# First projections of the retention layer: four whole tiles instead of five, the last tile's products bank by bank, banks emptied in a written order, decay tables behind

## The chip, the cores and the metric

The kernel runs on one core of a Trainium2 chip. The core has a matrix engine (TensorE, in the profile PE, its weight loads PEld), a vector engine (VectorE, DVE), a scalar engine (ScalarE, ACT), GpSimd (POOL) and SyncE (SP), which here issues nearly all transfers. Products land in eight banks of PSUM, which only PE, DVE and ACT reach. The metric is the device time of one execution in microseconds; lower is better.

## The reference

Two layers of a generator over latent tokens (256) with a context (256 tokens) through the same weights. Layer 0 mixes tokens by retention with four heads, layer 1 by neighbourhood attention; each is followed by a SwiGLU. The width is 1024. What matters here is the very beginning of layer 0: the adaLN modulation of the input and the projections of the first head.

```
m_lat = jnp.split(cond_lat @ ada_w[i] + ada_b[i], 6, axis=-1)
m_ctx = jnp.split(cond_ctx @ ada_w[i] + ada_b[i], 6, axis=-1)
a_lat = modulate(h_lat, m_lat[0], m_lat[1])
a_ctx = modulate(h_ctx, m_ctx[0], m_ctx[1])
...
q, k, v, g = jnp.split(a @ w_in, [hk, 2 * hk, 2 * hk + hv], axis=-1)
if rope is not None:
    q, k = apply_rope(q, *rope), apply_rope(k, *rope)
k = k * RET_DK ** -0.5
...
decay = lambda lg: jnp.broadcast_to(lg[None, :, None, None], (B, RET_HEADS, n, RET_DK))
```

Only latents are rotated (rope); the scan in both directions is computed as scores times a table of decays, then times the values, and the gate g goes through SiLU.

## The kernel before

**Tiles and operands.** The input stands transposed: eight tiles kt of 128 features by 512 tokens, 256 latents and then 256 of context. For each kt the program computes scale and shift of these 128 features for both streams, four passes of `ada.column` on DVE (L225: 1024 elements by the condition, summed into one column), then on ACT the modulated tile `am` (L408, one half per stream) and its rounded copy `aT[kt][0]` (L413). Products are made in float32r, an fp32 rounded so that PE takes it in one pass; to keep the precision, each operand is split into a high part (the rounded copy, made by ACT) and a low part (the rest, a subtraction on DVE), and a product is three of them: high by high, high by low, low by high (`mm3`, L138 to L142). `low(kt)` (L343) makes the low part of the input tile.

**First projections.** Weight unit kt (128 by 1024) of the first eight holds the first head's q and k columns (four blocks of 128) and v columns (512) for the features of tile kt. All eight banks are taken: `qk_ps[0..3]` for q (two) and k (two), transposed, and `v_ps[0..3]` for v, by tokens. Every tile adds to all eight banks, so no bank is final before the last tile. Tiles below `WHOLE`, which is 5, use the unsplit fp32 operands (`whole_products`, L345 to L354), one stream at a time, as soon as `am` is there. For the others ACT makes the high part of the weights (L402), DVE the low part (L359) and the input's low part, and `split_products` (L356 to L369) issues eight high by high products, one for each bank, and then the two others for each bank in turn. In the loop, the split products of tile kt − 1 stand behind the columns of tile kt. The last tile's stand behind the loop, and behind them the low parts of the whole tiles, which later projections need.

**Order.** `tc.manual_schedule` keeps the instructions written inside it in that order on the engines that it names; here all five. It ends after the low parts (L424). Everything else is ordered by the framework's scheduler, and `tc.issue_after(ins)` puts instructions of the same engine behind one. Loads on SP for the next tile are written at the top of each turn: adaLN rows, weights, input. Weight units share three buffers (`raw`), so a load waits until a buffer has been read. The stream of later units (`Stream`, L85 to L133) loads, casts on ACT (L123) and makes low parts on DVE (L124); unit 8 is the first of the gate projection.

**Behind the region, before.** Five tables are loaded (L426 to L430: distances `dlt`, decays `lg`, the cosines and sines, and the layer norms' columns), behind the weight load of tile 6. `decay_prep` and `decay_table` make for each head two tables of 128 by 384 decays: four exponentials on ACT (L457, L462), three products or sums on GpSimd (L458, L459, L463); heads 1, 2 and 3 are stored to DRAM (L465) and loaded again later, and head 0's stays in the one buffer `Dt`. They stand behind the last tile's cast (`lasts[-1]`). `qk_evac` empties two banks: four products with cosine and sine on DVE (L488), two copies of the context half on ACT (L493, L496), a difference and a sum (L497, L498), and the split. `v_evac` splits the four v banks. In the program's text the first head's q, k and v banks are emptied only after all functions have been defined, in front of `proj_g(0)`, the gate projection, whose first bank is one that has been emptied. Then come the scaled input z through the two buffers `pf` (L805, L806), which the decay tables use as well, and the heads: `scores`, where DVE multiplies by the table into `pf` (L554, L558), the next head's q and k, and `values`.

Of the kernel before, what the change touches and what calls it, by code (L numbers as in the profile page):

```python
# [8 lines left out]
F32 = mybir.dt.float32  # L9
F32R = mybir.dt.float32r  # L10
BF16 = mybir.dt.bfloat16
AF = mybir.ActivationFunctionType
ALU = mybir.AluOpType
# [5 lines left out]
P = 128  # L19
D = 1024  # L20
KT = D // P
NLAT = 256
NCTX = 256
NTOK = NLAT + NCTX
# [9 lines left out]
CTX_FIRST = (2, 3, 0, 1)  # L34
# [10 lines left out]
def backbone(ctx: ExitStack, tc: tile.TileContext, wpack, adapack, cond, condcol, xT, xtok, adab, lncol, lnrow,  # L45
# [271 lines left out]
    with Phase("ret", "yTh", "yTl", "vh", "vl", "kh", "kl") as rp:  # L317
# [17 lines left out]
            xts[kt] = rp.tile([P, NTOK], F32, tag=f"yT{'hl'[kt % 2]}{kt // 2 % 2}", name=f"xt{kt}")  # L335
            nc.sync.dma_start(xts[kt], xT[kt])

        WHOLE = 5
        ams = {}
        split_ops = {}  # L340

        def low(kt):
            nc.vector.tensor_tensor(out=aT[kt][1], in0=ams[kt], in1=aT[kt][0].bitcast(F32), op=ALU.subtract)  # L343
# [12 lines left out]
        def split_products(kt):  # L356

            raw, u = split_ops.pop(kt)
            nc.vector.tensor_tensor(out=u[1], in0=raw, in1=u[0].bitcast(F32), op=ALU.subtract)  # L359
            low(kt)  # L360
            outs = [(qk_ps[f], cut(u, slice(None), slice(f * P, f * P + P)), aT[kt]) for f in range(4)]
            outs += [(v_ps[t], cut(aT[kt], slice(None), slice(t * P, t * P + P)), cut(u, slice(None), slice(512, 1024)))
                     for t in CTX_FIRST]
            last = kt == KT - 1
            for o, x, m in outs:
                nc.tensor.matmul(o, x[0], m[0], start=False, stop=False)
            for o, x, m in outs:
                nc.tensor.matmul(o, x[0], m[1], start=False, stop=False)
                nc.tensor.matmul(o, x[1], m[0], start=False, stop=last)  # L369

        ORD = ("axw", "awx")
        REG = {PE, DVE, POOL, ACT, SP}
# [13 lines left out]
        for kt in range(KT):  # L386
            if kt + 1 < KT:
                for f in ORD[kt > 0]:
                    if f == "w":
                        stream.load_to(kt + 2)  # L390
                    elif f == "x":
                        load_x(kt + 1)
                    else:
                        ada.load_to(2 * kt + 4)

            am = ams[kt] = rp.tile([P, NTOK], F32, tag=f"v{'hl'[kt % 2]}{CTX_FIRST[kt // 2]}", name=f"am{kt}")
            raw = stream.raw.pop(kt)
            stream.split = stream.used = kt + 1
            if kt >= WHOLE:
                u = (wsplit.tile([P, UNIT], F32R, tag="whi", name=f"whi{kt}", bufs=stream.BUFS),  # L400
                     wsplit.tile([P, UNIT], F32R, tag="wlo", name=f"wlo{kt}", bufs=stream.BUFS))
                nc.scalar.copy(u[0], raw)  # L402
                split_ops[kt] = raw, u
            for s in range(2):
                sl = slice(s * NLAT, s * NLAT + NLAT)
                for i in (2 * kt, 2 * kt + 1):
                    ada.column(i, s)
                nc.scalar.activation(am[:, sl], xts[kt][:, sl], AF.Identity,  # L408
                                     bias=adacol[0][s][:, kt:kt + 1], scale=adacol[0][s][:, 8 + kt:9 + kt])
            ada.tiles.pop(2 * kt)  # L410
            ada.tiles.pop(2 * kt + 1)
            ada.done += 2
            lasts.append(nc.scalar.copy(aT[kt][0], am))  # L413
            if kt < WHOLE:
                whole_products(kt, raw)

            if kt - 1 in split_ops:
                split_products(kt - 1)
            if kt == WHOLE:
                tables_after = stream.last_load.ins  # L420
        split_products(KT - 1)
        for kt in range(WHOLE):
            low(kt)
        region.__exit__(None, None, None)  # L424
        with tc.issue_after(tables_after):
            nc.sync.dma_start(dlt, delta)  # L426
            nc.sync.dma_start(lg, decay.partition_broadcast(P))
            nc.sync.dma_start(cosT, rope[0])
            nc.sync.dma_start(sinT, rope[1])
            nc.sync.dma_start(lnc, lncol)  # L430

        dp = [rp.tile([P, 384], F32, tag=tg, name=f"dp{i}") for i, tg in enumerate(("g2", "yTl2", "sqsum"))]
        lgw = rp.tile([P, 2, 8], F32, name="lgw")

        def decay_prep():
            nc.scalar.activation(lg, lg, AF.Exp)
            nc.gpsimd.tensor_scalar(out=lg, in0=lg, scalar1=-1.0, scalar2=0.0, op0=ALU.mult, op1=ALU.add)
            nc.gpsimd.tensor_scalar(out=lgw[:, 0], in0=lg, scalar1=256.0, scalar2=0.0, op0=ALU.mult, op1=ALU.add)  # L440
            nc.gpsimd.tensor_scalar(out=lgw[:, 1], in0=lg, scalar1=-1.0, scalar2=0.0, op0=ALU.mult, op1=ALU.add)
            nc.scalar.activation(dp[0], dlt, AF.Relu)
            nc.scalar.activation(dp[1], dlt, AF.Relu, scale=-1.0)

            nc.gpsimd.memset(dp[2], 1.0)
            nc.gpsimd.affine_select(out=dp[2], in_=dp[2], compare_op=ALU.not_equal, fill=2.0, base=-128,
                                    pattern=[[1, 384]], channel_multiplier=-1)

        def load_decay(h):
            Dt[h] = rp.tile([P, 2, 384], F32, tag="Dt", name=f"Dt{h}")  # L450
            nc.sync.dma_start(Dt[h], dscr[h])

        def decay_table(h):
            D_ = rp.tile([P, 2, 384], F32, tag="Dt", name=f"Dw{h}")
            e = [rp.tile([P, 384], F32, tag=f"yT{'hl'[i]}3", name=f"de{i}_{h}") for i in range(2)]
            for i in range(2):
                nc.scalar.activation(e[i], dp[i], AF.Exp, scale=lg[:, 4 * i + h:4 * i + h + 1])  # L457
            nc.gpsimd.tensor_tensor(out=e[0], in0=e[0], in1=e[1], op=ALU.mult)  # L458
            nc.gpsimd.tensor_tensor(out=D_[:, 1, :], in0=e[0], in1=dp[2], op=ALU.mult)  # L459
            x = [rp.tile([P, NTOK], F32, tag="pf", name=f"dx{i}_{h}", bufs=2)[:, 0:384] for i in range(2)]  # L460
            for i, rate in enumerate((lg[:, h:h + 1], lgw[:, 1, 4 + h:5 + h])):
                nc.scalar.activation(x[i], dlt, AF.Exp, scale=rate, bias=lgw[:, 0, 4 * i + h:4 * i + h + 1])  # L462
            nc.gpsimd.tensor_tensor(out=D_[:, 0, :], in0=x[0], in1=x[1], op=ALU.add)  # L463
            if h:
                nc.sync.dma_start(dscr[h], D_)  # L465
            else:
                Dt[h] = D_

        with tc.issue_after(lasts[-1].ins):
            decay_prep()  # L470
            for h in (1, 2, 3, 0):
                decay_table(h)

        qk = {}
        vv = {}
        gg = {}
        yT = {}
        Pp = {}

        def qk_evac(h, which, ps):  # L480

            f = rp.tile([P, 2, NTOK], F32, tag="qf", name=f"qf{h}{which}", bufs=1)
            scale = 1.0 / 16.0 if which == "q" else 1.0
            m = [rp.tile([P, NLAT], F32, tag=f"rm{i}", name=f"rm{i}_{h}{which}") for i in range(2)]
            x = [f[:, i, 0:NLAT] for i in range(2)]

            def times(o, i, table):
                nc.vector.scalar_tensor_tensor(out=o, in0=ps[i][:, 0:NLAT], scalar=scale, in1=table, op0=ALU.mult,  # L488
                                               op1=ALU.mult)

            times(x[0], 0, cosT)
            times(m[1], 0, sinT)
            nc.scalar.activation(f[:, 0, NLAT:], ps[0][:, NLAT:], AF.Copy, scale=scale)  # L493
            times(x[1], 1, cosT)
            times(m[0], 1, sinT)
            nc.scalar.activation(f[:, 1, NLAT:], ps[1][:, NLAT:], AF.Copy, scale=scale)  # L496
            nc.vector.tensor_tensor(out=x[0], in0=x[0], in1=m[0], op=ALU.subtract)  # L497
            nc.vector.tensor_tensor(out=x[1], in0=m[1], in1=x[1], op=ALU.add)  # L498
            pr = (rp.tile([P, 2, NTOK], F32R, tag=f"{which}h", name=f"{which}h{h}"),
                  rp.tile([P, 2, NTOK], F32R, tag=f"{which}l", name=f"{which}l{h}"))  # L500
            split_into(pr, f)
            qk[(h, which)] = pr

        def v_evac(h, ps):
            for t in CTX_FIRST:
                pr = (rp.tile([P, 512], F32R, tag=f"vh{t}", name=f"vh{t}_{h}"),
                      rp.tile([P, 512], F32R, tag=f"vl{t}", name=f"vl{t}_{h}"))
                split_into(pr, ps[t])
                vv[(h, t)] = pr

        def proj_qk(h):
            for which in "qk":
# [280 lines left out]
        def fam_of(pool, tag="fam", w=256, bufs=2):  # L793
            return lambda n, i, name: pool.tile([P, w], F32, tag=tag, name=name, bufs=bufs)[:, :n]

        for i, w in ((0, "q"), (2, "k")):
            qk_evac(0, w, qk_ps[i:i + 2])
        v_evac(0, v_ps)
        proj_g(0)
        for t in CTX_FIRST:  # L800
            for half in range(2):
# [605 lines left out]
```

## Time and profile before

| | |
|---|---|
| median of 3 runs | 1184.1 us (1179.56 to 1184.3) |
| profiled execution | 1185.73 us, its span 1184.0 us |
| mean granted clock of PE | 0.993 of full speed |
| busy: PE, PEld, DVE, ACT, POOL | 1157.6, 963.9, 785.0, 455.3, 291.8 us |
| all weight loads | 228 of 512 KB, median 3.7 us from issue to landing |

A row of a timeline gives the start in the span, the duration, the engine, the line of the kernel, the operation, what it writes and reads with partitions and elements, and how many were merged; in brackets the idle time of the engine before it and what ended that. A row of the list of waits gives who waited for whom, the total, how often, and the longest. A row of a window gives its stretch and length, the busy time and count of each engine asked for, the granted clock of PE, the share of the transfer engines, and GB/s. A matmul's duration holds its pipeline; from start to start it is shorter.

### The profile page before, as it was taken

Reading aid. Unit: us, or ns where it says so; the run is one execution under the profiler, and the core shown is the slowest. Engines: PE = TensorE matmul, PEld = TensorE weight load, DVE = VectorE, ACT = ScalarE, POOL = GpSimd, SP = SyncE. Lnnn points to the kernel's source line nnn. Section 1 sums busy time; section 2 is a strip of 40 time slices with the busy share of each in tenths; the row PEclk is TensorE's granted clock in tenths of the full one; section 3 lists DMA queues with packets and bytes.
Section 4 is the critical chain, followed back from the end, with each engine's and each line's share of the span. In section 5 each row is a group of like instructions: output and inputs, shape, how many; then the busy total and the mean of one; then the engine's idle time right before and its main releaser. Section 6 shows DMA issues by size and latency. Waiting matters only on the chain. (4 is left out here: it accounts for less than half of the span.)

```text
span 1184.0 us, 15315 instructions
## 1 busy us (share of the span) xinstructions
PE 1157.6 (98%) x5670; PEld 963.9 (81%) x5670; DVE 785.0 (66%) x1131; ACT 455.3 (38%) x714; POOL 291.8 (25%) x281
## 2 busy tenths in 40 slices
PE   7999999999999998999999999999999998999997
PEld 5778888888888887888888888887888877888886
DVE  7987957645745589667776476555355577778645
ACT  3582423332433253232212233135354465566530
POOL 0054214104203567000131000015444434300000
PEclk9999999999999999999999999999999999999999
DMA  8755554233334223456546677426488743777650
GB/s 325 275 204 209 161 196 138 90 126 128 133 107 131 83 72 110 170 103 246 205 163 208 173 261 246 148 67 128 152 224 258 205 140 117 245 232 224 209 170 36
DMA packets 70010, 201.72 MB, mean 170 GB/s; under 512 B 14512, under 2 KB 17072, under 8 KB 69936
## 3 DMA queue, kind: packets, MB, share of 16 engines
q1 hardware_dynamic: 69648, 200.23, 53.0%
q8 instruction: 44, 0.72, 0.3%
q10 hardware_dynamic: 288, 0.52, 0.1%
q14 instruction: 30, 0.25, 0.1%
HBM read 187.98 MB, written 2.25 MB: 161 GB/s over the span
## 5 line engine op out<-in xcount | busy, mean ns | idle before, releaser
L124 DVE TENSOR_TENSOR wlo<-raw,whi 128x1024 fp32r<-128x1024 f32 x220 | 289.5, 1320 | 209.2 <-ACT whi L123 202.8
L123 ACT CAST whi<-raw 128x1024 fp32r<-128x1024 f32 x220 | 229.7, 1049 | 462.9 <-PE f L141 122.8
L225 DVE CUSTOM_DVE_ANT_0 junk<-adaraw,cond,adab_sb 128x1024 bf16<-128x1024 f32 x160 | 216.4, 1352 | 48.8 <-DMA adaraw<-in_adapack 46.3
L141 PE MATMUL f<-aT,whi 128*128 128x512 f32 (+1 forms) x384 | 143.7, 374 | 4.8 <-DVE aT L756 4.7
L142 PE MATMUL f<-aT,wlo 128*128 128x512 f32 (+1 forms) x384 | 143.3, 373 | 0.0
L140 PE MATMUL f<-aT,whi 128*128 128x512 f32 (+1 forms) x384 | 143.1, 373 | 0.0
L851 PE MATMUL f<-aT,whi 128*128 128x512 f32 x320 | 112.9, 397 | 0.0
L313 POOL TENSOR_TENSOR pb_n<-pa_n,mhalf 128x1 f32<-128x1 f32 x12 | 8.4, 702 | 347.8 <-DVE pa_n L312 347.8
L852 PE MATMUL f<-aT,wlo 128*128 128x256 f32 x320 | 90.0, 282 | 0.3 <-DVE wlo L124 0.3
L141 PEld LDWEIGHTS f<-aT,whi 128*128 128x128 f32 x384 | 72.9, 190 | 18.2 <-DVE aT L756 5.5
L140 PEld LDWEIGHTS f<-aT,whi 128*128 128x128 f32 x384 | 73.0, 190 | 12.6
L142 PEld LDWEIGHTS f<-aT,wlo 128*128 128x128 f32 x384 | 73.0, 190 | 12.5
L851 PEld LDWEIGHTS f<-aT,whi 128*128 128x128 f32 x320 | 60.0, 188 | 14.4
L140 PE MATMUL d<-whi,hh 128*128 128x512 f32 x176 | 68.6, 389 | 0.0
L142 PE MATMUL d<-whi,hl 128*128 128x512 f32 x176 | 68.5, 389 | 0.0
L141 PE MATMUL d<-wlo,hh 128*128 128x512 f32 x176 | 68.5, 389 | 0.0
L142 PE MATMUL v<-whi,aT 128*128 128x512 f32 x160 | 63.0, 395 | 1.8 <-POOL aT L756 1.8
L622 POOL TENSOR_TENSOR z<-t,z 128x512 f32<-128x512 f32 x28 | 44.4, 1595 | 76.0 <-DVE t L620 75.9
L140 PE MATMUL v<-whi,aT 128*128 128x512 f32 x160 | 62.8, 393 | 0.0
L141 PE MATMUL v<-wlo,aT 128*128 128x512 f32 x160 | 62.8, 392 | 0.0
L852 PEld LDWEIGHTS f<-aT,wlo 128*128 128x128 f32 x320 | 60.3, 189 | 0.8 <-DVE wlo L124 0.7
L140 PE MATMUL g<-aT,whi 128*128 128x512 f32 x128 | 50.7, 396 | 1.9 <-ACT qf0q L493 1.9
(286 smaller groups left out, 2436.8 us busy)
## 6 DMA issues: line engine op xcount, KB each, us to landing
raw<-in_wpack SPq DMA_DIRECT2D x228, 512.0 KB, 3.7
adaraw<-in_adapack SPq DMA_DIRECT2D x96, 512.0 KB, 4.5
ln<-in_lnrow SPq DMA_DIRECT2D x16, 256.0 KB, 4.5
braw<-in_rpb SPq DMA_DIRECT2D x8, 512.0 KB, 5.3
kh<-sth SPq DMA_DIRECT2D x32, 128.0 KB, 3.0
kl<-stl SPq DMA_DIRECT2D x32, 128.0 KB, 2.4
gateb<-gscr SPq DMA_DIRECT2D x6, 512.0 KB, 6.3
xt<-in_xT SPq DMA_DIRECT2D x8, 256.0 KB, 4.6
```

Source lines behind the costliest of these rows:

```text
L123: nc.scalar.copy(hi, raw)
L124: self.last_low = nc.vector.tensor_tensor(out=lo, in0=raw, in1=hi.bitcast(F32), op=ALU.subtract)
L140: nc.tensor.matmul(o, s[0], m[0], start=start, stop=False)
L141: nc.tensor.matmul(o, s[0], m[1], start=False, stop=False)
L142: nc.tensor.matmul(o, s[1], m[0], start=False, stop=stop)
L225: nc.vector.tensor_tensor_reduce(out=junk, in0=self.tiles[i], in1=condb[s], scale=1.0, scalar=adab_sb[:, l, m:m + 1], op0=ALU.mult, op1=AL ...
L313: nc.gpsimd.tensor_tensor(out=b, in0=a, in1=mhalf[:, 0:n], op=ALU.pow)
L622: eng.tensor_tensor(out=z[t][:, cs], in0=t2, in1=z[t][:, cs], op=ALU.add)
L851: nc.tensor.matmul(b[i].rearrange("p (a t) -> p a t", a=2), st[0], m, start=kt == 0, stop=False)
L852: nc.tensor.matmul(b[i][:, 0:NLAT], st[1], m[:, 0, :], start=False, stop=kt == KT - 1)
```

## The change

`WHOLE` becomes 4: tile 4 is split as well, and its split products stand behind the columns of tile 5. The last tile's products are issued bank by bank, all three of one bank in a row, in the order q, q, k, k, v of tokens 2, 3, 0, 1. The table loads move into the loop, behind the loads for tile 7 and with units 8 and 9 ahead of the columns of the norms. The region goes on after the last products with an order written out: unit 8's split, the low parts of the four whole tiles, `decay_prep`, the table of head 1, and the two q banks; between q's copies and its sums stand the four v banks and unit 9's split. The tables of heads 2, 3 and 0 come behind q's second copy on ACT. The k banks are emptied outside the region, as before.

```
-        WHOLE = 5
+        WHOLE = 4
...
             last = kt == KT - 1
+            if last:
+                for o, x, m in outs:
+                    mm3(o, x, m, False, True)
+                return
...
-        def qk_evac(h, which, ps):
+        def qk_evac(h, which, ps, between=None):
...
-            nc.scalar.activation(f[:, 1, NLAT:], ps[1][:, NLAT:], AF.Copy, scale=scale)
+            copy = nc.scalar.activation(f[:, 1, NLAT:], ps[1][:, NLAT:], AF.Copy, scale=scale)
+            if between:
+                between(copy)
...
-            if kt == WHOLE:
-                tables_after = stream.last_load.ins
+            if kt == KT - 2:
+                nc.sync.dma_start(dlt, delta)
+                nc.sync.dma_start(lg, decay.partition_broadcast(P))
+                nc.sync.dma_start(cosT, rope[0])
+                nc.sync.dma_start(sinT, rope[1])
+                stream.load_to(KT + 2)
+                nc.sync.dma_start(lnc, lncol)
         split_products(KT - 1)
+        stream.split_to(KT + 1)
         for kt in range(WHOLE):
             low(kt)
+        decay_prep()
+        decay_table(1)
+        decay_after = []
+        def first_values(copy):
+            v_evac(0, v_ps)
+            stream.split_to(KT + 2)
+            decay_after.append(copy.ins)
+        qk_evac(0, "q", qk_ps[0:2], first_values)
         region.__exit__(None, None, None)
-        with tc.issue_after(tables_after):
-            nc.sync.dma_start(dlt, delta)
...
-        with tc.issue_after(lasts[-1].ins):
-            decay_prep()
-            for h in (1, 2, 3, 0):
+        with tc.issue_after(decay_after[0]):
+            for h in (2, 3, 0):
                 decay_table(h)
...
-        for i, w in ((0, "q"), (2, "k")):
-            qk_evac(0, w, qk_ps[i:i + 2])
-        v_evac(0, v_ps)
+        qk_evac(0, "k", qk_ps[2:4])
         proj_g(0)
```

`decay_prep`, `decay_table`, `load_decay`, `v_evac` and the rest of `qk_evac` move up in the text, unchanged.

More of the change, by code (lines that the diff above doesn't have):

```diff
@@ L368, in split_products, with decay_prep @@
                 nc.tensor.matmul(o, x[0], m[1], start=False, stop=False)
-                nc.tensor.matmul(o, x[1], m[0], start=False, stop=last)
+                nc.tensor.matmul(o, x[1], m[0], start=False, stop=False)
+        dp = [rp.tile([P, 384], F32, tag=tg, name=f"dp{i}") for i, tg in enumerate(("g2", "yTl2", "sqsum"))]
+        lgw = rp.tile([P, 2, 8], F32, name="lgw")
+        def decay_prep():
+            nc.scalar.activation(lg, lg, AF.Exp)
+            nc.gpsimd.tensor_scalar(out=lg, in0=lg, scalar1=-1.0, scalar2=0.0, op0=ALU.mult, op1=ALU.add)
+            nc.gpsimd.tensor_scalar(out=lgw[:, 0], in0=lg, scalar1=256.0, scalar2=0.0, op0=ALU.mult, op1=ALU.add)
+            nc.gpsimd.tensor_scalar(out=lgw[:, 1], in0=lg, scalar1=-1.0, scalar2=0.0, op0=ALU.mult, op1=ALU.add)
+            nc.scalar.activation(dp[0], dlt, AF.Relu)
+            nc.scalar.activation(dp[1], dlt, AF.Relu, scale=-1.0)
+            nc.gpsimd.memset(dp[2], 1.0)
+            nc.gpsimd.affine_select(out=dp[2], in_=dp[2], compare_op=ALU.not_equal, fill=2.0, base=-128,
+                                    pattern=[[1, 384]], channel_multiplier=-1)
@@ new lines, in load_decay, with decay_table @@
+        def load_decay(h):
+            Dt[h] = rp.tile([P, 2, 384], F32, tag="Dt", name=f"Dt{h}")
+            nc.sync.dma_start(Dt[h], dscr[h])
+        def decay_table(h):
+            D_ = rp.tile([P, 2, 384], F32, tag="Dt", name=f"Dw{h}")
+            e = [rp.tile([P, 384], F32, tag=f"yT{'hl'[i]}3", name=f"de{i}_{h}") for i in range(2)]
+            for i in range(2):
+                nc.scalar.activation(e[i], dp[i], AF.Exp, scale=lg[:, 4 * i + h:4 * i + h + 1])
+            nc.gpsimd.tensor_tensor(out=e[0], in0=e[0], in1=e[1], op=ALU.mult)
+            nc.gpsimd.tensor_tensor(out=D_[:, 1, :], in0=e[0], in1=dp[2], op=ALU.mult)
+            x = [rp.tile([P, NTOK], F32, tag="pf", name=f"dx{i}_{h}", bufs=2)[:, 0:384] for i in range(2)]
+            for i, rate in enumerate((lg[:, h:h + 1], lgw[:, 1, 4 + h:5 + h])):
+                nc.scalar.activation(x[i], dlt, AF.Exp, scale=rate, bias=lgw[:, 0, 4 * i + h:4 * i + h + 1])
+            nc.gpsimd.tensor_tensor(out=D_[:, 0, :], in0=x[0], in1=x[1], op=ALU.add)
+            if h:
+                nc.sync.dma_start(dscr[h], D_)
+            else:
+                Dt[h] = D_
@@ new lines, in backbone, with times @@
+        qk = {}
+        vv = {}
+        gg = {}
+        yT = {}
+        Pp = {}
+        def qk_evac(h, which, ps, between=None):
+            f = rp.tile([P, 2, NTOK], F32, tag="qf", name=f"qf{h}{which}", bufs=1)
+            scale = 1.0 / 16.0 if which == "q" else 1.0
+            m = [rp.tile([P, NLAT], F32, tag=f"rm{i}", name=f"rm{i}_{h}{which}") for i in range(2)]
+            x = [f[:, i, 0:NLAT] for i in range(2)]
+            def times(o, i, table):
+                nc.vector.scalar_tensor_tensor(out=o, in0=ps[i][:, 0:NLAT], scalar=scale, in1=table, op0=ALU.mult,
+                                               op1=ALU.mult)
+            times(x[0], 0, cosT)
+            times(m[1], 0, sinT)
+            nc.scalar.activation(f[:, 0, NLAT:], ps[0][:, NLAT:], AF.Copy, scale=scale)
+            times(x[1], 1, cosT)
+            times(m[0], 1, sinT)
+            copy = nc.scalar.activation(f[:, 1, NLAT:], ps[1][:, NLAT:], AF.Copy, scale=scale)
+            if between:
+                between(copy)
+            nc.vector.tensor_tensor(out=x[0], in0=x[0], in1=m[0], op=ALU.subtract)
+            nc.vector.tensor_tensor(out=x[1], in0=m[1], in1=x[1], op=ALU.add)
+            pr = (rp.tile([P, 2, NTOK], F32R, tag=f"{which}h", name=f"{which}h{h}"),
+                  rp.tile([P, 2, NTOK], F32R, tag=f"{which}l", name=f"{which}l{h}"))
+            split_into(pr, f)
+            qk[(h, which)] = pr
@@ L371, in backbone, with v_evac @@
+        def v_evac(h, ps):
+            for t in CTX_FIRST:
+                pr = (rp.tile([P, 512], F32R, tag=f"vh{t}", name=f"vh{t}_{h}"),
+                      rp.tile([P, 512], F32R, tag=f"vl{t}", name=f"vl{t}_{h}"))
+                split_into(pr, ps[t])
+                vv[(h, t)] = pr
         ORD = ("axw", "awx")
@@ L437, in decay_prep @@
[L437 to L467, printed above, removed]
@@ L469, in backbone @@
-        with tc.issue_after(lasts[-1].ins):
-            decay_prep()
-            for h in (1, 2, 3, 0):
-                decay_table(h)
[L474 to L478, printed above, removed]
-        def qk_evac(h, which, ps):
[L482 to L495, printed above, removed]
-            nc.scalar.activation(f[:, 1, NLAT:], ps[1][:, NLAT:], AF.Copy, scale=scale)
[L497 to L502, printed above, removed]
```

12 lines of the change are left out of this document (removed).

## The prediction

> **What bounds the kernel now.** I read the page's busy shares first, then who waited for whom on TensorE, then the timeline of each engine between 30 and 120 us, because the change touches nothing outside that stretch. The page:
>
> ```profile
> PE 1157.6 (98%) x5670; PEld 963.9 (81%) x5670; DVE 785.0 (66%) x1131; ACT 455.3 (38%) x714; POOL 291.8 (25%) x281
> ```
>
> TensorE (PE) is busy in 98% of the span. So a change shortens the kernel by what it takes off PE: work, idle time, or time at a low clock. Of the list of PE's waits one row lies in the changed code:
>
> ```profile
> PE g L140 <- ACT qf0q L493: 1.9, 1, 1.9
> ```
>
> PE's timeline shows where, and how long each tile takes before it:
>
> ```profile
> 33.10 1.89 PE L351 MATMUL qk<-am,raw 128*128 128x256 f32 x8
> ...
> 39.99 1.89 PE L351 MATMUL qk<-am,raw 128*128 128x256 f32 x8
> ...
> 46.47 1.49 PE L366 MATMUL qk<-aT,whi 128*128 128x512 f32 x4
> ...
> 52.34 1.07 PE L366 MATMUL qk<-aT,whi 128*128 128x512 f32 x4
> ...
> 57.78 1.07 PE L366 MATMUL qk<-aT,whi 128*128 128x512 f32 x4
> ...
> 62.99 0.39 PE L369 MATMUL v<-whi,aT 128*128 128x512 f32 x1
> 65.32 0.51 PE L140 MATMUL g<-aT,whi 128*128 128x512 f32 x1 [1.94 <-ACT qf0q L493]
> ...
> 88.80 0.40 PE L140 MATMUL S<-qh,kh 128*128 128x512 f32 x1
> ```
>
> The reader is to see three things. A whole tile (tile 3) takes 39.99 − 33.10 = 6.89 us. A split tile (tile 6) takes 57.78 − 52.34 = 5.44 us for 24 products, 0.2267 each. And all eight banks are full until the last product ends at 62.99 + 0.23 = 63.22; the gate projection, which needs a free bank, starts at 65.32, when the first q bank has been read. That is 2.10 us from end to start (the trace calls 1.94 of it idle). The 96 gate products would take 96 × 0.2267 = 21.76 us, yet from 65.32 to the scores at 88.80 there are 23.48: 1.72 us more. The granted clock (the column after the busy times) says why, in one-microsecond windows:
>
> ```profile
> 64.00:65.00 1.00, 0.00 (x0) 1.00 1.06 344
> 66.00:67.00 1.00, 1.00 (x4) 0.50 1.02 340
> ```
>
> After the gap PE runs at half clock for a while. The gap costs 2.10 + 1.72 = 3.82 us in all.
>
> **The change, part by part.**
>
> **Tile 4 becomes a split tile.** PE saves 6.89 − 5.44 = 1.45 us. VectorE (DVE) has to make the low parts of tile 4's weights and input before tile 6's adaLN columns, not later. DVE's timeline:
>
> ```profile
> 37.67 1.28 DVE L225 CUSTOM_DVE_ANT_0 junk<-adaraw,cond,adab_sb 128x1024 bf16<-128x1024 f32 x1
> ...
> 39.59 1.28 DVE L225 CUSTOM_DVE_ANT_0 junk<-adaraw,cond,adab_sb 128x1024 bf16<-128x1024 f32 x1 [0.63 <-DMA adaraw<-in_adapack]
> ...
> 44.79 1.22 DVE L359 TENSOR_TENSOR wlo<-raw,whi 128x1024 fp32r<-128x1024 f32 x1
> 45.93 0.69 DVE L343 TENSOR_TENSOR aT<-am,aT 128x512 fp32r<-128x512 f32 x1
> 46.53 1.28 DVE L225 CUSTOM_DVE_ANT_0 junk<-adaraw,cond,adab_sb 128x1024 bf16<-128x1024 f32 x1
> ...
> 51.72 1.22 DVE L359 TENSOR_TENSOR wlo<-raw,whi 128x1024 fp32r<-128x1024 f32 x1
> ...
> 55.73 4.53 DVE L343 TENSOR_TENSOR aT<-am,aT 128x512 fp32r<-128x512 f32 x6
> 60.19 4.00 DVE L124 TENSOR_TENSOR wlo<-raw,whi 128x1024 fp32r<-128x1024 f32 x2
> 64.11 0.41 DVE L488 SCALAR_TENSOR_TENSOR qf0q<-qk,cosT 128x256 f32<-128x256 f32 x1
> 64.44 0.41 DVE L488 SCALAR_TENSOR_TENSOR rm_0q<-qk,sinT 128x256 f32<-128x256 f32 x1
> ```
>
> DVE is full here but for 0.63 us of waiting at 39.59. A pair of low parts takes 46.53 − 44.79 = 1.74 us (1.14 and 0.60); a tile's four columns take 44.79 − 39.59 = 5.20. Tile 5's columns end at 37.67 + 1.21 = 38.88, the distance of two passes without the accumulator's read. From there, after the change: low parts of tile 4, 38.88 to 40.62; columns of tile 6, to 45.82 (their rows have landed at 39.59); low parts of tile 5, the second from 46.96, done at 46.96 + 0.69 = 47.65; columns of tile 7, 47.56 to 52.75; low parts of tile 6, done at 52.75 + 1.14 + 0.69 = 54.58.
>
> PE against that: tile 3 ends at 39.99. Tile 4 runs to 45.43 (its low parts are there at 40.71, after the first eight products they are wanted at 41.80). Tile 5's eight high products run to 47.24, then PE waits 0.41 for the low part and ends at 47.65 + 16 × 0.2267 = 51.28. Tile 6's high products run to 53.09, then a wait of 1.49 to 54.58, end 58.21. Tile 7 ends at 63.65. So the saving of 1.45 turns into two new waits of 1.90 together: PE ends 0.43 us **later** than before. VectorE is what sets this stage. The ends for the waits are 0 (PE then ends at 61.75) and the 1.90 computed; I take 1.90, since each duration stands in a row and DVE executes in order.
>
> Do the loads allow it? SyncE's timeline:
>
> ```profile
> 40.18 0.33 SPq L109 DMA_DIRECT2D raw<-in_wpack  x1
> ...
> 41.08 0.86 SPq L217 DMA_DIRECT2D adaraw<-in_adapack  x2
> ...
> 46.04 0.33 SPq L109 DMA_DIRECT2D raw<-in_wpack  x1
> ```
>
> Tile 7's adaLN rows (41.08) were used from 46.53 without a wait, and now from 47.56: 1 us of room. Tile 7's weights, issued at 46.04 when tile 5's weights had been read, find tile 4's buffer free from 40.1 on, and go out right behind those rows. What queues up behind them on SyncE is new: five table loads (before at about 42 to 44.5, ahead of tile 7), then weight units 8 and 9, which wait for tiles 5 and 6 to be read (47, 54). Unit 8 lands about 3.7 us after 47, by the page's row:
>
> ```profile
> raw<-in_wpack SPq DMA_DIRECT2D x228, 512.0 KB, 3.7
> ```
>
> It is wanted on ScalarE behind tile 7's cast at 54.0, so it is early. Unit 10 may now go out behind the first table's store at about 63; with 3.7 of flight, 1.05 for the cast and up to 2.0 for the low part it is ready near 71, and the gate projection wants it at 63.65 + 2 × 5.44 = 74.5. Cost of all loads: nothing; if that cover were gone, PE would wait one for one.
>
> **The last tile goes bank by bank.** No product is added. The first q bank is now final after three products, 58.21 + 0.68 = 58.89, not at the end.
>
> **The banks are emptied in a fixed order.** From 54.49 DVE has two weight low parts (1.14 each), tile 7's and four more input low parts (0.60 each): 5.28 us, to 59.8. Before, six inputs and two weights (5.88 by the same prices) took 64.11 − 55.73 = 8.38 beside GpSimd's table products; with that factor, 1.43, it is 62.0. Then the two table products of the first bank, 0.33 apart and 0.41 long: 60.5 to 62.8. ScalarE's copy follows the second one, and it must be free:
>
> ```profile
> 54.35 1.28 ACT L438 ACT_TABLE_LOAD   x1
> ...
> 58.33 0.60 ACT L457 ACTIVATE de<-dp,lg 128x384 f32<-128x384 f32 x1
> ...
> 64.89 0.38 ACT L493 ACTIVATE qf0q<-qk 128x256 f32<-128x256 f32 x1 [0.43 <-DVE rm_0q L488]
> ```
>
> From its table load to the last of the first decay table's exponentials but one took 3.98 us; with a unit's cast (1.05) ahead and that exponential (0.5) behind, ScalarE is through at about 54.0 + 1.05 + 3.98 + 0.5 = 59.5. The copy ends at 60.9 to 63.2. The bank is wanted at 63.65. So the gate projection follows without a gap, with 0.4 to 2.8 us to spare, and what is late next is the second q bank, wanted 5.44 us later. The 2.10 us gap goes, and the half clock behind it, 1.72.
>
> **Sum.** +0.43 − 2.10 − 1.72 = −3.39: the scores start at 63.65 + 21.76 = 85.41, not at 88.80.
>
> **Does a new PE wait trip the clock?** Two other gaps in front of PE:
>
> ```profile
> 432.69 0.39 PE L141 MATMUL f<-aT,whi 128*128 128x256 f32 x1 [1.67 <-DVE aT L756]
> 433.00:434.00 1.00, 1.00 (x11) 1.00 0.09 35
> 992.12 1.09 PE L778 MATMUL T<-ident,z 128*128 128x128 f32 x8 [1.52 <-DVE z L710]
> 993.00:994.00 1.00, 1.00 (x7) 1.00 0.97 369
> ```
>
> Gaps of 1.67 and 1.52 us left the clock at 1.00, that of 1.94 did not. The new 1.49 is below both, so I price the clock at nothing, the other end being 1.72. The Trainium skill (TensorE: Matmul & The Clock Gate, "Why this matters for your kernels") puts the bound at idle gaps of about 3 us. By it the gap before the gates should not have halved the clock, and the sum would be only +0.43 − 2.10 = −1.67, an estimate from that page; the windows at 66 us contradict it, and the measurement decides.
>
> **Does the gain last?** The score products wait for decay tables and, through shared buffers, for GpSimd's loads of x:
>
> ```profile
> 61.22 1.89 POOL L459 TENSOR_TENSOR Dw<-de,dp 128x384 f32<-128x384 f32 x1
> ...
> 82.77 1.99 POOL L463 TENSOR_TENSOR Dw<-dx,dx 128x384 f32<-128x384 f32 x1
> 102.62 1.31 DVE L554 TENSOR_TENSOR pf<-S,Dw 128x512 f32<-128x512 f32 x2 [4.38 <-POOL z L806]
> 109.53 2.31 POOL L150 TENSOR_TENSOR pl<-pf,ph 128x256 fp32r<-128x256 f32 x2 [1.94 <-ACT ph L149]
> 114.77 0.39 PE L140 MATMUL O<-ph,vh 128*128 128x512 f32 x1
> ...
> 116.48 0.28 PE L140 MATMUL O<-ph,vh 128*128 128x256 f32 x1
> ```
>
> The last score operand is done at 111.84, and PE wanted it at 116.48; 3.39 earlier it wants it at 113.09. That leaves 1.25 us. The first table is done at 63.11 now, and by the ScalarE sum above about as late after the change, so this chain stays, and the gain with it.
>
> **The rivals.** *The clock drops in tile 6.* The 1.49 us wait plus the 0.41 before it add up to 1.90, as much as the gap that tripped it. Against: 4.3 us of dense work lie between them. Price 1.72: −1.67.
>
> *The first bank is not free in time*, so the change doesn't do what it says: unit 8's load waits for tile 6's buffer instead of tile 5's, lands at 54.6 + 3.7, and everything on ScalarE and DVE behind its cast moves by about 3.3 us, the copy to 64.2 or later, up to 66.5. Then the gap and the half clock come back, and only the 0.43 stays: no gain. For: DVE's 62.8 leaves little. Against: the buffer order worked out above.
>
> *The tables come too late: slower.* Tables 2, 3 and 0 may start on ScalarE only behind the second q copy, among v casts and a silu table. In the trace the whole chain from 61.22 over 82.77 to 111.84 is serial. Each microsecond beyond 1.25 is an idle PE before the value products; from 1.25 + 3.39 = 4.64 us of lateness on, the kernel is slower than before. If the three tables each lose 2 us to ScalarE's queue the chain is 6 late, PE waits 4.75, more than the 1.94 that halves the clock (1.72): −3.39 + 4.75 + 1.72 = +3.1. Against: between tables GpSimd waits for the store of the one before, which hides part of ScalarE's time.
>
> *No wait on VectorE in tiles 5 and 6*: −3.39 − 1.90 = −5.3.
>
> **How the numbers follow.** The profiled execution took 1185.73 us (span 1184.0); 3.4 less is 1182.3. The median of the three runs shown is 1184.1, 1.6 lower, so on its scale: forecast 1180.7, chance 0.55; clock drop 1182.4, 0.13; bank late 1184.5, 0.12; tables late 1187.2, 0.08; no waits 1178.8, 0.12. The range is 1177.8 to 1185.0: it takes in all but the late tables, with 1 us below the best case for what moves elsewhere. A measurement of this kernel tells about 0.5%, 5.9 us, from no change. Only the best case with some luck behind it passes 1178.2: 0.13. Slower by 5.9 needs tables some 9 us late: 0.05. Within: 0.82.
>
> **What would show it.** PE: tile 4's split products from about 40, waits of about 0.4 and 1.5 us inside tiles 5 and 6 released by DVE's aT, tile 7 ending near 63.7, gate products directly behind it at a granted clock of 1.00, scores near 85.4. DVE: no idle time between 20 and 60. The forecast is wrong if a PE wait stands before the gates or before the value products, if the clock column shows 0.50 between 50 and 90, or if DVE's chain ends tile 6 at another time than 54.6.

## The result, and the profile after

| | before | changed |
|---|---|---|
| median of 20 executions each | 1182.82 us (1178.46 to 1186.47) | 1187.11 us (1179.33 to 1189.8) |
| ratio | | 1.0031, 95% interval 1.002 to 1.0043 |
| profiled execution | 1185.73 us, span 1184.0 | 1180.52 us, span 1178.7 |
| mean granted clock in it | 0.993 | 0.996 |

The changed kernel is 0.3% slower, above the range of the prediction. Two more sets of 12 executions of the very same changed kernel gave 0.9998 (0.9977 to 1.0019) and 1.0019 (1.0005 to 1.0034). The profiled execution is one of the quickest of its set, 6.6 us below the median, so the two profiles must not be subtracted as they stand: the causes are to be found by stages, and tested on repeats. Two later executions of the kernel before, one of 2792.92 us and one at a mean clock of 0.947, are left out of the averages of the clock below.

The busy times, and the first rows of PE's list of waits after the change (who waited for whom, total, how often, longest):

```profile
PE 1153.2 (98%) x5670; PEld 961.1 (82%) x5670; DVE 784.1 (67%) x1132; ACT 457.2 (39%) x715; POOL 290.8 (25%) x281
```

```profile
PE qk L372 <- DVE aT L343: 2.0, 2, 1.2
...
PE O L141 <- POOL pl L150: 1.4, 1, 1.4
```

The wait of the gates is gone. The two waits on VectorE are the predicted ones. The wait of the value products (O) is new. PE's timeline after the change:

```profile
38.69 1.50 PE L370 MATMUL qk<-aT,whi 128*128 128x512 f32 x4
...
47.45 0.50 PE L372 MATMUL qk<-aT,whi 128*128 128x512 f32 x1 [0.89 <-DVE aT L343]
...
54.38 0.50 PE L372 MATMUL qk<-aT,whi 128*128 128x512 f32 x1 [1.16 <-DVE aT L343]
...
58.18 0.39 PE L140 MATMUL qk<-aT,whi 128*128 128x512 f32 x1
...
63.39 0.39 PE L142 MATMUL v<-whi,aT 128*128 128x512 f32 x1
63.62 0.39 PE L140 MATMUL g<-aT,whi 128*128 128x512 f32 x1
...
85.38 0.40 PE L140 MATMUL S<-qh,kh 128*128 128x512 f32 x1
...
113.20 0.39 PE L140 MATMUL O<-ph,vh 128*128 128x256 f32 x1
115.02 0.39 PE L141 MATMUL O<-pl,vh 128*128 128x256 f32 x1 [1.43 <-POOL pl L150]
```

Tile 7 ends and the scores come where the prediction had them, to a few hundredths: the gates start 0.23 behind the last product of tile 7, and the scores come at 85.38 (before 88.80). Then PE stands for 1.43 us in the middle of the value products. The windows behind the gates' start, and those where the clock dropped before:

```profile
64.00:65.00 1.00, 1.00 (x7) 1.00 0.69 273
66.00:67.00 1.00, 1.00 (x6) 1.00 0.00 0
```

The clock column (after the busy share) is 1.00 in both, where before it read 0.50 at 66. VectorE after the change:

```profile
46.70 0.69 DVE L343 TENSOR_TENSOR aT<-am,aT 128x512 fp32r<-128x512 f32 x1
...
53.63 0.69 DVE L343 TENSOR_TENSOR aT<-am,aT 128x512 fp32r<-128x512 f32 x1
...
57.11 2.83 DVE L343 TENSOR_TENSOR aT<-am,aT 128x512 fp32r<-128x512 f32 x4
59.86 0.41 DVE L426 SCALAR_TENSOR_TENSOR qf0q<-qk,cosT 128x256 f32<-128x256 f32 x1
```

and ScalarE:

```profile
60.70 0.39 ACT L431 ACTIVATE qf0q<-qk 128x256 f32<-128x256 f32 x1 [1.08 <-DVE rm_0q L426]
```

Tile 6's low part ends at 54.32, and the first bank is free at 61.09, 2.5 us before the gates want it.

**Where the gain goes.** The last score operand is GpSimd's `pl`:

```profile
108.62 1.65 POOL L150 TENSOR_TENSOR pl<-pf,ph 128x256 fp32r<-128x256 f32 x1 [0.36 <-ACT ph L149]
113.22 1.74 POOL L150 TENSOR_TENSOR pl<-pf,ph 128x256 fp32r<-128x256 f32 x1 [2.95 <-ACT ph L149]
```

It is done at 114.96 now, 3.12 us later than the 111.84 of before, although the scores come 3.42 earlier. VectorE shows why. Before, the last two products with the decay table stand together, and the second head's q, already in the banks, behind them:

```profile
108.60 0.74 DVE L558 TENSOR_TENSOR pf<-S,Dw 128x256 f32<-128x256 f32 x2
...
110.47 0.42 DVE L488 SCALAR_TENSOR_TENSOR qf1q<-q,cosT 128x256 f32<-128x256 f32 x1
```

After the change the framework's scheduler, which orders all that stands behind the written region, has put four other steps between the two (two sums of the second head's q, a low part of the weights and a column of the modulation):

```profile
107.69 0.41 DVE L574 TENSOR_TENSOR pf<-S,Dw 128x256 f32<-128x256 f32 x1
108.02 0.52 DVE L438 TENSOR_TENSOR qf1q<-rm_1q,qf1q 128x256 f32<-128x256 f32 x1
108.46 1.21 DVE L124 TENSOR_TENSOR wlo<-raw,whi 128x1024 fp32r<-128x1024 f32 x1
109.60 1.76 DVE L225 CUSTOM_DVE_ANT_0 junk<-adaraw,cond,adab_sb 128x1024 bf16<-128x1024 f32 x1
...
111.28 0.41 DVE L437 TENSOR_TENSOR qf1q<-qf1q,rm_1q 128x256 f32<-128x256 f32 x1
111.62 0.41 DVE L574 TENSOR_TENSOR pf<-S,Dw 128x256 f32<-128x256 f32 x1
```

and on ScalarE the cast of the second head's q ahead of the last score cast:

```profile
111.79 1.05 ACT L149 CAST qh<-qf1q 128x1024 fp32r<-128x1024 f32 x1 [3.25 <-DVE qf1q L437]
112.75 0.40 ACT L149 CAST ph<-pf 128x256 fp32r<-128x256 f32 x1
```

That is 3.60 us on VectorE (from 108.02, where the step behind `pf` begins, to the next `pf` at 111.62) and about 1 us on ScalarE. With the slack of 1.25 this delays PE by 3.12 − 1.25 = 1.87; from the first value product to the next stage the changed kernel takes 1.92 more than before (10.29 against 8.37).

**And the rest of the difference between the two profiles** is no part of the change. Of the 5.21 us by which PE's last product comes earlier, 1.49 are there when the second head's scores start (187.86 against 189.35), and 3.84 arise around 431 to 454, in layer norms long behind the change. There the execution before happened to wait twice more and to drop its clock, and the one after did not; repeats of the changed kernel and variants of both show it either way.

### The profile page after: what moved, and what is told of

It is laid out like the page before. It is cut to its first block, busy times and chain, and to the rows that moved or that the text cites. A ratio compares the mean times of both kernels' runs of the same rounds, so it can differ in the third digit from the quotient of the medians.

```text
span 1178.7 us, 15314 instructions
## 1 busy us (share of the span) xinstructions
PE 1153.2 (98%) x5670; PEld 961.1 (82%) x5670; DVE 784.1 (67%) x1132; ACT 457.2 (39%) x715; POOL 290.8 (25%) x281
## 5 line engine op out<-in xcount | busy, mean ns | idle before, releaser
L142 PE MATMUL v<-whi,aT 128*128 128x512 f32 x164 | 64.6, 395 | 1.8 <-POOL aT L772 1.8
L140 PE MATMUL v<-whi,aT 128*128 128x512 f32 x164 | 64.2, 391 | 0.0
```

The costliest lines, as they stand in the source:

```text
L140: nc.tensor.matmul(o, s[0], m[0], start=start, stop=False)
L142: nc.tensor.matmul(o, s[1], m[0], start=False, stop=stop)
```

## The experiments

Each ran in 12 executions beside 29 to 35 of the kernel before, on the same chip. The times of one set spread by 4 to 13 us, so beside each ratio stands a stretch of the trace: from the first projection product to the second head's scores, 179.07 us before and 177.83 in the first trace after. All traces agree behind that point, but for a few places that vary from execution to execution, whatever the variant.

**The changed kernel again** (no edit).

> The changed kernel once more, for a second trace, since the first is of an execution of 1180.5 us and the median is 1187. Theory A (clock): the waits of about 1 to 1.5 us that the change leaves in front of TensorE, in tiles 5 and 6 and before the value products near 115, lie close to where the clock is halved; in a usual execution one or two of them pass it. Then the trace, if its execution is near 1187, shows the granted clock at 0.50 for some 3.4 us behind 47, 54 or 115, where the first trace has 1.00, and the scores or the end of the value products come 1.7 us or more later than in the first trace. Rival B (later stages): everything up to 135 us is as in the first trace, and the 6 us are lost behind it, at 430 to 460 or near 800 or 990. Time against the kernel before: 1.002 to 1.005.

1185.54 against 1185.03 us, ratio 0.9998 (0.9977 to 1.0019). The stretch took 179.43, the waits in tiles 5 and 6 were 1.31 and 1.19, and the value products waited twice:

```profile
114.93 0.38 PE L140 MATMUL O<-ph,vh 128*128 128x256 f32 x1 [1.05 <-ACT ph L149]
116.75 0.38 PE L141 MATMUL O<-pl,vh 128*128 128x256 f32 x1 [1.43 <-POOL pl L150]
```

So the wait at O is no accident of one trace, and may be larger: O to the next stage took 3.01 more than before. The gain at the gates was all there (the gates followed without a gap), and was gone at 114.

**Five whole tiles, all else changed.**

```
-        WHOLE = 4
+        WHOLE = 5
```

> All of the change but the fourth tile: five whole tiles again. The waits inside tiles 5 and 6 should go (low parts come 1.06 us earlier against PE and PE 1.45 later), and the last tile should end near 63.2, the scores start near 85.0. Theory A: if it is the waits in tiles 5 and 6 that trip the clock, the time falls by 2 to 6 us against the changed kernel, to 0.997 to 1.000 of the kernel before. Rival B or a trip at the value products: no better than the changed kernel, 1.001 to 1.005.

1188.59 us, ratio 1.0017 (0.9998 to 1.0036). The waits in tiles 5 and 6 shrink to one of 0.17. From the first product to the scores it took 74.62 against 75.35 (after), so four whole tiles cost about 0.7 us there, not 0.43; but from the scores to O it took 26.59 against 25.98, so that about 0.1 is left of it. It did not help the total: the wait at O was 0.69 and 1.43, and the clock halved behind it, 4.15 us more than before in that stage. The loss is not in tiles 4 to 6.

**The kernel before with four whole tiles.**

```
-        WHOLE = 5
+        WHOLE = 4
```

> The kernel before with four whole tiles and nothing else. By the prediction's sum the two waits eat the saving (+0.4 us) and the gap before the gates stays: 1.000 to 1.001, scores near 89.2. Theory A with the trip in tiles 5 and 6: 1.7 to 3.4 us more, 1.002 to 1.003, and half clock behind 54.

1183.81 us, ratio 0.9981 (0.9962 to 1.0001). Waits of 0.48 and 1.17 appear, and the gap before the gates stays; yet the clock did not drop behind it:

```profile
66.47 0.50 PE L140 MATMUL g<-aT,whi 128*128 128x512 f32 x1 [1.71 <-ACT qf0q L493]
```

```profile
66.00:67.00 1.00, 0.53 (x2) 1.00 0.90 242
68.00:69.00 1.00, 1.00 (x6) 1.00 1.05 418
```

No wait stood at O. So four whole tiles alone do not make the value products wait; the new order does, since all three sets of the changed kernel and the two variants that leave out one other part of it (above and below) wait there.

**The last tile's products not bank by bank.**

```
-            if last:
-                for o, x, m in outs:
-                    mm3(o, x, m, False, True)
-                return
...
-                nc.tensor.matmul(o, x[1], m[0], start=False, stop=False)
+                nc.tensor.matmul(o, x[1], m[0], start=False, stop=last)
```

> All of the change but the last tile's order: its eight high products first, then the two others bank by bank as before. The first bank is then final at about 58.2 + 1.81 + 0.45 = 60.5, not at 58.9, still 3.2 us before the last product, so the gate projection should start without a gap or with one of up to 1 us: 0 to +1 us against the changed kernel, 1.002 to 1.005 of the kernel before, if rival B or the value products are the cause. Theory A says the same, so this run only tells how much the order of the last tile is worth.

1187.69 us, ratio 1.0015 (0.9997 to 1.0032). The gates still follow tile 7 without a gap (63.72 to 63.94): with all eight high products first, the first bank is final seven products, 7 × 0.2267 = 1.59 us, later, and that is within the 2.5 us of room. What bank by bank does buy is the k bank: the scores wait 0.78 for `kl` here, and from the scores to O it took 27.07 against 25.98. At O the waits were 0.75 and 1.43. So it is the written order behind the last products that takes the gap away, and the order of the last tile's products adds little.

**Own buffers for the rows of x, in the changed kernel.** The loads of x share two buffers (`pf`) with the decay tables and the score products; here they get four others, which the first two score operands do not use (the last two do, and come behind x in them).

```
-                xr = rp.tile([P, 512], F32, tag="pf", name=f"xr{t}{half}", bufs=2)
+                xr = rp.tile([P, 512], F32, tag=f"yT{'hl'[half]}{t % 2}", name=f"xr{t}{half}")
```

> The changed kernel; the eight loads of x for z take four buffers that lie idle since the first tiles, in place of the two that they share with the decay tables and the score products. Theory C (order of the queue): the change gains 3.8 us up to the scores and TensorE gives 1.9 to 3.0 of them back waiting for the last score operand, since VectorE's and ScalarE's queues now hold other work between the last two score products. Without the sharing the score products should come before the next head's q work, the wait before the value products goes, and from the first tile's start to the second head's scores it takes about 175.9 us (177.8 and 179.4 in the two traces of the changed kernel, 179.1 in that of the kernel before). Time 0.997 to 0.999 of the kernel before. Rival B (later stages, the clock's chance): the stretch may shorten, but the time stays at 1.000 to 1.002.

1181.33 against 1183.67 us, ratio 0.9988 (0.9963 to 1.0013). The wait at O is gone: the stage took 8.37, as before, and the last `pl` is done at 105.69, 8.4 us ahead of the first value product:

```profile
104.25 1.44 POOL L150 TENSOR_TENSOR pl<-pf,ph 128x256 fp32r<-128x256 f32 x2
```

The stretch took 177.90, not the 175.9 that was expected. What is saved at O was lost ahead of it: the first tile took 9.81 us on PE (8.40 in the first trace), VectorE waited 2.08 us at 36.18 for adaLN rows, PE waited 1.19 and 1.16 in tiles 5 and 6, and the scores came 77.33 us behind the first product instead of 75.35.

**The same in the kernel before.**

> The same buffers in the kernel before. There TensorE does not wait at the value products, and both theories expect nothing: 0.999 to 1.001, the gap before the gates stays at about 1.9 us, the way from the first tile to the second head's scores at 177 to 179 us.

1183.89 us, ratio 0.9991 (0.9973 to 1.0009): no difference that can be told, and the stage at O is unchanged at 8.37. Here, where the operands are not late, the buffers are worth nothing. The gap before the gates was 1.79 here, and halved the clock:

```profile
68.00:69.00 1.00, 1.00 (x4) 0.53 1.00 410
69.00:70.00 1.00, 1.00 (x3) 0.50 1.03 332
```

**Own buffers and five whole tiles.** Both edits above, in the changed kernel.

> The changed kernel with the buffers for x and with five whole tiles. The waits inside tiles 5 and 6 go as well: last product of tile 7 about 0.7 us earlier after the first tile's start than in the changed kernel, first tile to second scores about 175.2 us by theory C. Time 0.996 to 0.999 of the kernel before, the best of the four.

1181.8 us, ratio 0.9981 (0.9961 to 1.0001). No wait at O; one of 1.20 in tile 6, in an execution in which VectorE waited 2.88 us at 42.41 for adaLN rows; the stretch took 177.92, not the expected 175.2. Against four whole tiles with the same buffers nothing can be told.

**The second head's q behind the last score operand.**

```
+                if (h, which) == (1, "q"):
+                    with tc.issue_after(last_pf[0].ins):
+                        qk_evac(h, which, ps)
...
+                    last_pf[h] = nc.vector.tensor_tensor(out=pf[:, :n], in0=b[:, :n], in1=Dt[h][:, 1, off:off + 256],
```

> The changed kernel with its buffers as they are, and one edge: the work that empties the second head's q banks on VectorE stands behind the last score product of the first head. By theory C that alone takes most of the wait: ScalarE's cast of the last scores no longer stands behind the cast of q, so the last operand comes some 1.5 us earlier, and TensorE's wait before it falls from 1.43 to at most 0.5 us. First tile to second scores 176 to 178 us. Time 0.998 to 1.000 of the kernel before. If the wait stays, it was not the order but the shared buffers.

1182.54 against 1183.67 us, ratio 0.9984 (0.9964 to 1.0004). The edge changes nothing but the order of the queues. The wait at O fell to 0.42:

```profile
114.79 0.39 PE L141 MATMUL O<-pl,vh 128*128 128x256 f32 x1 [0.42 <-POOL pl L150]
```

and the stage took 0.70 more than before instead of 1.92 to 3.95; the stretch took 176.54. On VectorE, though, the last two score products stand as far apart as without the edge, 3.92 us from start to start (3.93 in the first trace):

```profile
109.16 0.41 DVE L580 TENSOR_TENSOR pf<-S,Dw 128x256 f32<-128x256 f32 x1
...
113.08 0.41 DVE L580 TENSOR_TENSOR pf<-S,Dw 128x256 f32<-128x256 f32 x1
```

The sums of q are gone from between them, but a low part and a column, 3.58 us together, stand there. What the edge saved lies behind the last product: ScalarE's cast starts 0.44 us after that product's start (1.13 in the first trace, behind the cast of q), and GpSimd's `pl` takes 0.73 us in place of 1.74. What was left comes by GpSimd:

```profile
106.27 0.62 POOL L827 TENSOR_SCALAR z<-xr 128x512 f32<-128x512 f32 x1 [2.63 <-DMA xr<-in_xtok]
...
114.01 0.73 POOL L150 TENSOR_TENSOR pl<-pf,ph 128x256 fp32r<-128x256 f32 x1 [1.95 <-ACT ph L149]
```

It waited 2.63 us for a row of x in the shared buffers, and VectorE's second score product waited with it, so the two causes, order and buffers, work on the same operand.

**Both repairs beside the changed kernel.** The changed kernel a third time, both edits, and both with five whole tiles, on one chip.

> The changed kernel once more, to stand on the same chip beside the two below. If the wait before the value products is what keeps the gain from lasting, its trace shows the scores near 85.4 to 86.0, a wait of 1.4 us or more at the first value products released by GpSimd's pl, and the second head's scores 177.8 to 179.9 us behind the first projection product; its time is 1.000 to 1.003 of the kernel before. If that wait has no part in it, its time is no different from the two kernels below.

> The changed kernel with both repairs: the scaled input has buffers of its own, and the second head's q banks are emptied behind the last score operand of the first head. If the order of the queues in front of the value products is what gives the gain back, no TensorE wait stands there, the second head's scores come 175.2 to 176.6 us behind the first projection product (179.07 before), and the time is 2 to 3.5 us below the kernel before: 0.997 to 0.998. If the gain is lost elsewhere, or to the clock whatever the waits, the time is 0.999 to 1.002 and equal to the changed kernel beside it.

> The same with five whole tiles, so without the two waits on VectorE in tiles 5 and 6 but with one longer tile on TensorE. If those waits cost no more than the prediction's sum says (1.90 us against 1.45 us saved), this is 0.4 us faster than the one with four whole tiles at equal clock, which these rounds cannot tell apart: 0.9965 to 0.998. If the two waits also cost clock now and then, it is faster by 1 us or more.

Against 1182.37 us before: the changed kernel 1184.7 (1.0019, 1.0005 to 1.0034), with both repairs 1179.61 (0.9985, 0.9968 to 1.0001), with five whole tiles as well 1179.88 (0.9988, 0.9973 to 1.0003). Against the changed kernel itself the repaired one is at 0.9961, with a 95% interval of 0.9947 to 0.9974 (means of the 12 executions each, 1180.04 and 1184.70, and their spread): 4.7 us, the clearest difference of the study. The changed kernel waited 0.43 and 1.43 at O, and PE's windows behind it show a dropped clock:

```profile
116.00:117.00 1.00, 1.00 (x6) 0.85 0.03 8
117.00:118.00 1.00, 1.00 (x5) 0.50 0.15 25
118.00:119.00 1.00, 1.00 (x7) 0.50 0.86 303
```

That stage cost 3.95 more than before, and the stretch took 179.86. In the repaired kernel the last score operand is done at 103.61, 8.8 us ahead of the first value product:

```profile
102.18 1.43 POOL L150 TENSOR_TENSOR pl<-pf,ph 128x256 fp32r<-128x256 f32 x2
```

and O follows without a wait; the stretch took 176.87, 2.20 less than before. That missed the 175.2 to 176.6 that were expected by 0.3: this execution's first tile took 9.72 us on PE, 0.67 longer than that of before (8.38 to 9.90 in all traces). The ratio came out above the expected 0.997 to 0.998 as well, 0.9985, with an interval that holds both. Five whole tiles save 0.63 up to the scores (75.67 against 76.30) but lose 0.60 behind them, with 26.59 against 25.99 from the scores to O: no difference remains.

## Why the prediction was wrong

**Tile 4 as a split tile: right.** Predicted waits 0.41 and 1.49, together 1.90; measured 0.89 and 1.16, together 2.05, with tile 4 starting at 38.69 in place of 39.99: the sum is right, each of the two is off by 0.3 to 0.5. That the earlier start gained nothing bears out that VectorE sets this stage: its low part of tile 6 was done at 54.32 (predicted 54.58), and in the third set, with a first tile as long as in the trace of before (9.08 and 9.05 us), the gates start at 63.63 all the same. The end of tile 7, 63.39 + 0.23 = 63.62, was forecast at 63.65. In other executions with four whole tiles the two together were 1.4 to 2.5.

**Loads: right for PE and for this trace.** No PE wait on a weight load appeared anywhere in this stretch. But VectorE, which sets the stage, waited for adaLN rows between 20 and 60 us in six of the ten traces with the new order, by 0.47 to 3.12 us together (0.48 to 1.28 in the three without it). Where it did not wait and four tiles are whole, the scores come 75.28 to 75.35 us behind the first product, against the predicted 75.13; where it waited longest with four, 77.33.

**Bank by bank and the emptying order: right.** VectorE worked on the first bank from 59.86 to 60.60 (predicted 60.5 to 62.8, so sooner than worked out), ScalarE's copy ended at 61.09, and the gap went. The rival in which the bank comes too late did not happen, in any of the traces. That the written order and not the products bank by bank does it, the prediction did not separate.

**The sum up to the scores: right.** 85.38 against 85.41. The last tenths are luck: counted from the first product, which came 0.25 us earlier than in the trace of before, it is 75.35 against 75.13. In all ten traces with the new order PE went into the gates without a gap, and the half clock behind the gap went too. One term was taken as certain and is not: the half clock of 1.72 stood in the trace of before and in that with own buffers (gap 1.79), but not in that with four whole tiles (gap 1.71).

**Does the gain last: here the prediction failed.** The step reads: "The first table is done at 63.11 now, and by the ScalarE sum above about as late after the change, so this chain stays, and the gain with it." The chain of tables did stay: the last table was done at 84.66 (84.76 before) and the first score product on VectorE began at 102.68 (102.62). But the last operand was not done at 111.84; it was done at 114.96, and in other executions later. The prediction followed the transfers and the tables and took the order of VectorE's and ScalarE's queues behind the region as given. It is not given: the scheduler made a new one, with 3.60 us of other work in front of the last score product on VectorE and the cast of q in front of the last score cast on ScalarE. The repair by one edge, which changes the order alone, took the wait down to 0.42, though not by way of VectorE, where other work filled the place. With own buffers the last score product starts 15.08 us behind the first scores on PE instead of 26.24, and the wait went. How much of it is order alone and how much the shared buffers is not settled; that the wait stands on these two is shown. So 1.92, 3.01 and 3.95 us in the three traces went back, of a predicted gain of 3.39 (3.17, 2.66 and 3.18 up to the scores, counted from the first product). The rival of late tables had the place right (an idle PE before the value products) and the cause wrong.

**Does a new wait trip the clock: the rule was wrong.** The prediction read a threshold for one gap, between 1.67 and 1.94 us, out of three gaps. The trace of before itself speaks against it: there the clock dropped at 451.39 as well, with no single gap above 1.38 us in the 3.41 us ahead. What counts is the idle time summed over a fixed stretch: see the last section. The waits in tiles 5 and 6 never dropped the clock, as it said; the new wait at O did in two of the five traces in which it was 1.4 us or more.

**The total.** The predicted 1180.7 was worked out from a gain of 3.4. (Of the chances, the 0.13 for a time below 1178.2 is more than the 0.12 of the only case that could reach it.) In the stretch up to the second head's scores the three traces of the changed kernel (177.83, 179.43, 179.86) average 179.04, against 179.07 in the one trace of before: no gain. Counted from the second tile, since the first varies, they are 169.43, 170.87 and 170.78 against 170.02, and 167.15 with both repairs. The first comparison shows 0.31%, 3.7 us, more than that, the two repeats −0.2 and +2.2 by their ratios. What of this is left is not settled. One part can be seen in every execution: its mean granted clock. The time lost to it, (1 − clock) × span, which counts each stretch at half clock by half, averaged 6.3, 5.7 and 5.8 us in the three sets of the changed kernel and 5.0, 4.8 and 4.0 in three sets of the kernel before, with standard errors of 0.3 to 0.6; with both repairs 3.7. (In each trace 1.8 to 3.0 us of it lie at the very end, behind PE's last product.) So the changed kernel loses about 1 us more to the clock although the gap before the gates is gone, and the wait at O accounts for part of that, as the two executions show. Where the rest falls, the few traces cannot say.

## What to carry to other kernels

A change that starts a stage earlier must be followed to the last operand of the next stage, through the queue of every engine on the way, and where a scheduler orders what lies behind a written region, the order of before is no forecast of the order after. When a gain at one gap vanishes, look for the next wait of the same engine, then for what stands between two instructions that used to be neighbours; an edge and separate buffers may give it back, as here (4.7 us against the changed kernel; against the kernel before the interval of the repaired one, 0.9968 to 1.0001, still holds no difference). When a profiled execution can be 7 us from the median, compare by stages and on repeats, not by totals.

## What the runs showed of the hardware that was not expected

**The clock drop depends on where idle time falls, not on the length of one gap.** The layer norm near 431 leaves PE idle for 1.66 or 1.67 us in all 13 traces; the clock halved behind it in four of them (the changed kernel twice, and once each in two variants), for about 3.4 us, which costs 1.5 to 1.7. The changed kernel's first repeat and its first trace, PE's windows:

```profile
433.00:434.00 1.00, 1.00 (x5) 0.61 0.01 2
434.00:435.00 1.00, 1.00 (x7) 0.50 0.55 172
```

```profile
433.00:434.00 1.00, 1.00 (x10) 1.00 0.76 225
434.00:435.00 1.00, 1.00 (x11) 1.00 1.11 326
```

Same gap, same code, half the products in the second window of the one. What differs is the place of the gap on a grid. Within each trace all drops begin a whole number of 3.413 us apart: in the trace of before at 65.68, 451.39 and 806.37, which is 113.0 and then 104.0 such stretches. With the trace cut into these stretches, PE's busy time in four of them (the trace of before; four whole tiles in the kernel before; the changed kernel's third set; its second):

```profile
62.27:65.68 3.41, 1.47 (x7) 1.00 0.51 153
62.94:66.35 3.41, 1.81 (x9) 1.00 0.37 120
113.29:116.70 3.41, 1.58 (x7) 1.00 0.59 228
112.37:115.78 3.41, 1.89 (x10) 1.00 0.98 333
```

The first and the third, idle for 1.94 and 1.83 us, were followed by half clock; the second and the fourth, idle for 1.60 and 1.52, were not, although the fourth's execution waited for 2.48 us in two pieces: the grid cuts them. In all 13 traces, from 26 us to 6 us before the end, each of the nine stretches with 1.74 us or more of idle time was followed by half clock, ten of the 19 with 1.58 to 1.73 were, and none with less. What decides between 1.58 and 1.73 stays open. Of the gaps before the gates, 1.94 and 1.79 dropped the clock and 1.71 did not; of the waits at O in two pieces, 2.48 and 2.18 did not, 1.86 and 2.12 did. The Trainium skill (TensorE: Matmul & The Clock Gate, "Why this matters for your kernels") puts the bound at idle gaps of about 3 us; here gaps well below it drop the clock in some executions. The place of the grid differs from trace to trace, so for one gap the drop remains a chance: a gap of 1.7 us is best priced at itself plus a third of 1.7, an estimate from the four of 13.

**Unchanged stages vary between executions.** ScalarE's `pt` copies in layer 1 make PE wait near 890 not at all in some traces and 1.35 to 2.82 us in others, the changed kernel and variants of both among them; the layer norms at 431 to 454 differ by up to 3.84 us. This, and not the change, made most of the 5.2 us between the first two profiles.
